# Products with the tokens on the output's partitions: 512 columns at a time from chunks of half the rows

## The chip, the cores and the metric

The kernel runs on one core of a Trainium2 chip. The metric is the device time of one execution in microseconds (us). TensorE (PE) multiplies, VectorE (DVE) and ScalarE (ACT) evaluate and convert, GpSimd (POOL) does some element-wise work, SyncE (SP) issues most of the DMAs.

## The reference, cut to what matters

Two layers of a hybrid network run over 256 tokens (`x`) and 256 context tokens (`ctx`); layer 0 updates both, layer 1 only the first. All products are 1024 wide on the reduced side (`D_MODEL = 1024`).

```python
mod = silu(c) @ ada_w[i] + ada_b[i]            # 6 * 1024 columns
h   = modulate(rmsnorm(x, norm1_g), sh1, sc1)
p   = h @ w_in                                 # 7168 columns:
# u, v of the gating (512 + 512), q, k, v of attention (3 * 512),
# three parts of the long convolution (3 * 512), three gates (3 * 1024)
a    = u * (w_s @ rmsnorm(v) + b_s)            # gating over tokens
attn = softmax(q k^T + bias) v                 # 8 heads of 64
hy   = two long convolutions, by Fourier transforms
m    = g_a * (a @ wb0) + g_b * (attn @ wb1) + g_c * (hy @ wb2)
x    = x + g1 * (m @ w_out)
x    = x + g2 * (gelu(conv(h2 @ up_a)) * (h2 @ up_b)) @ down
```

## The kernel before

Nearly every product is done with the features on the output's partitions: a piece of the weight, 128 x 128, is the stationary operand, and all tokens (512 in layer 0, 256 in layer 1) stream past it. To keep fp32 accuracy each operand is split in a high and a low part (ACT casts the high part, L251, DVE subtracts, L258), and three matmuls are made for each piece: low times high, high times high, high times low (L311 to L313). Tiles of the split weights are called `wp`, those of the activations `hh` and `hl`, the accumulators `mm`.

Two products are made the other way round, with the tokens on the partitions: `v` of the gating (4 tiles of 128 tokens in layer 0, 2 in layer 1) and `v` of attention (`va`, 4 tiles in both). There the activations are stationary and the weights stream (`tm_use`, L940 to L957, accumulators `mt`, L951 to L953). A load brings 1024 rows by 256 columns of the weight, so a tile takes 24 matmuls of 256 columns, and ACT writes each half of 256 columns out (L954).

The order of the work is written out by hand. `items` is a list of weight chunks (`dense`), of the chunks of the modulation's weights (`native`, function `ada`, L373: one chunk is 128 rows by 2048 columns, used as it is, and makes four matmuls of 512 columns) and of calls. `run_items` (L222) walks through it, loads three chunks ahead, and splits the weights `AHEAD` = 4 (layer 0) or 6 parts ahead. A chunk is cut into parts by `cuts` (L209).

Beside this list run the side works: gating (`sgu`), the filters, the convolution (`hyena`), attention. Each is a generator whose steps are pieces of work. They wait in the queue `side`, and `pump` (L155) makes one step of the first of them. In layer 0 a step is made after every accumulated tile of 512 tokens: 24 matmuls for a gate or a q, k tile, 12 for a tile of a branch product (L329: `ctl["pace"]`), after two tiles of `tm_use`, and after every `ada`. So it is the list that spaces the steps of the side works. The attention's loop (L848) makes one of six kinds of step in turn: in steps 0, 1, 3 and 5 of six it makes `scores` (matmuls `S`, then on DVE a bias, the maximum `mx`, on ACT the exponential, on DVE the division, giving two tiles `P_`); in steps 2 and 4 `stack` prepares the next heads' `K_` and `Q_` by turns on ACT and DVE; one step after its scores, `P_` is transposed by TensorE (`PT`); later `values` multiplies (`pv`). I count these steps from 0 in layer 0.

The chunk of `ada` with ch = 1 takes 8 of these units and the one with ch = 2 another 8, all in layer 0. Before the change they stand behind the six chunks of the convolution's parts, behind the four chunks of q and k, behind the two of `va`, and behind the first four gates. An `ada` chunk holds one of the four accumulator buffers (pool `psm`) from its first unit to its eighth. The gates and the branch products alternate (`LEAD` = 2 gates ahead).

Of the kernel before, what the change touches and what calls it, by code (L numbers as in the profile page):

```python
# [11 lines left out]
F32 = mybir.dt.float32  # L12
F32R = mybir.dt.float32r
AF = mybir.ActivationFunctionType
# [5 lines left out]
KD = 8  # L20
# [73 lines left out]
def trunk_kernel(ctx: ExitStack, tc: tile.TileContext, A: dict, out: bass.AP):  # L94
    nc = tc.nc
    mm, act, vec, pool = nc.tensor.matmul, nc.scalar.activation, nc.vector, nc.gpsimd
# [5 lines left out]
    psm = ctx.enter_context(tc.tile_pool(name="psm", bufs=4, space=PSUM))  # L102
# [3 lines left out]
    def U(name, dt=F32):  # L106
        return unit.tile([128, 512], dt, tag="u", name=name)

    def fm(name, n, T, dt=F32):

        if T == 512:
            return [U(name, dt) for _ in range(n)]
        r = []
        for _ in range((n + 1) // 2):
            u = U(name, dt)
            r += [u[:, 0:256], u[:, 256:512]]
        return r[:n]
# [37 lines left out]
    def pump(n=1):  # L155
        for _ in range(n):
            if not side:
                return
            try:
                next(side[0])  # L160
            except StopIteration:
                side.popleft()
# [8 lines left out]
    def start(g):  # L171
        side.append(g)
        return g
# [32 lines left out]
    def dense(src, kt, ncols, use, kind="m"):  # L206
        items.append((kind, src, kt, ncols, use))

    def cuts(kind, kt, ncols):  # L209


        if kind == "m":
            return [[(k, min(k + 4, kt), c, c + 128) for k in range(0, kt, 4)] for c in range(0, ncols, 128)]
        return [[(k, k + 2, 0, ncols) for k in range(0, kt, 2)]]

    def native(src, use):
        items.append(("n", src, 0, 0, use))

    def call(f, wait=True):
        items.append(("c", None, wait, 0, f))  # L220

    def run_items():  # L222
# [4 lines left out]
        for n, i in enumerate(loads):  # L227
            for j, ps in enumerate(cuts(*items[i][0:1], *items[i][2:4])):
                parts += [(n, i, q) for q in ps]
                last[i, j] = len(parts)  # L230
# [44 lines left out]
        for i, it in enumerate(items):  # L275
            if it[0] == "c":
                if it[2]:
                    flush()
                it[4]()
                continue  # L280
            if it[0] == "n":
                if i not in raw:
                    load_native()
                it[4](raw.pop(i))
                load_native()
                continue
            load_to(pos + RAWB + (not nats))
            qs = cuts(it[0], it[2], it[3])

            def piece(j, more=True, i=i, qs=qs):  # L290

                n = last[i, j]
                ahead = ctl["ahead"] if more else 0
                hi_to(n + ahead + (2 if more else 0))
                advance()
                lo_to(n + ahead)
                ctl["at"] = n
                W = []
                for m, (k0, k1, c0, c1) in enumerate(qs[j]):
                    h, l_ = spl.pop(n - len(qs[j]) + m)  # L300
                    W += [(h[:, k], l_[:, k]) for k in range(k1 - k0)]
                return W
            it[4](piece)
            pos += 1
# [30 lines left out]
    def fm_chunk(R, segs, evac, nm=2):  # L335

        def use(piece):
            for m in range(nm):
                W = piece(m)
                for (s0, s1) in segs:  # L340
                    fm_run([(W, evac, m)], R, s0, s1)
        return use
# [30 lines left out]
    def ada(l, ch, k):  # L373
        src = A["ada_w"][l, k * 128:(k + 1) * 128, ch * 2048:(ch + 1) * 2048]

        def use(w):
            if k == 0:
                ada.ps = psm.tile([128, 512], F32, tag="m", name="ada")
            ps = ada.ps
            v = w.rearrange("p (t j i) -> p j t i", j=4, i=32)  # L380
            for j in range(4):
                mm(ps[32 * j:32 * j + 32, :], lhsT=scc[:, k, :], rhs=v[:, j], start=(k == 0), stop=(k == KD - 1),  # L382
                   tile_position=(0, 32 * j))
            if k == KD - 1:
                ada_evac(l, ch, ps)
            pump()
        native(src, use)
# [33 lines left out]
    def ada_evac(l, ch, ps):  # L421

        tr = U("adat")
        vec.transpose(out=tr, in_=ps)
        t0 = ch * 16
        b = prm[:, P_AB + 48 * l + t0:P_AB + 48 * l + t0 + 16].unsqueeze(2).to_broadcast([128, 16, 2])
        vec.tensor_tensor(out=mod[l][:, t0:t0 + 16, :], in0=tr.rearrange("p (t i) -> p t i", i=32)[:, :, 0:2], in1=b,
                          op=ALU.add)
        if ch != 1:
            w_, g_ = (0, P_N1) if ch == 0 else (1, P_N2)  # L430
            sc = mod[l][:, 8 + 24 * w_:16 + 24 * w_, :]
            g = prm[:, g_ + 8 * l:g_ + 8 * l + 8].unsqueeze(2).to_broadcast([128, KD, 2])
            vec.scalar_tensor_tensor(out=gs[l][:, w_], in0=sc, scalar=1.0, in1=g, op0=ALU.add, op1=ALU.mult)
# [442 lines left out]
    def layer(l):  # L876
        nseg = 2 if l < DEPTH - 1 else 1
        T = 256 * nseg
        full = [(0, T)]
        S = {}  # L880
        w_in = A["w_in"][l].rearrange("(k p) n -> p k n", p=128)

        def col(c0, n=256):
            return w_in[:, :, c0:c0 + n]
# [35 lines left out]
        def late(f):  # L920

            def use(piece):
                f()(piece)
            return use
# [12 lines left out]
            else:  # L937
                dense(col(c * 256), KD, 256, late(lambda c=c: fm_edge(S["H"], halves, u_evac(c), 2, st1, 4, NH1[1])))

        def tm_use(c, ntt, dst, func):  # L940

            def use(piece):
                W = piece(0)
                rh, rl = S["H"]
                for t in range(ntt):
                    ps = psm.tile([128, 512], F32, tag="m", name="mt")
                    o = ps[:, 0:256]
                    for k in range(KD):
                        wh, wl = W[k]
                        x, y = rh[k][:, t * 128:(t + 1) * 128], rl[k][:, t * 128:(t + 1) * 128]  # L950
                        mm(o, lhsT=x, rhs=wl, start=(k == 0), stop=False)  # L951
                        mm(o, lhsT=x, rhs=wh, start=False, stop=False)  # L952
                        mm(o, lhsT=y, rhs=wh, start=False, stop=(k == KD - 1))  # L953
                    act(out=S[dst][t][:, c * 256:(c + 1) * 256], in_=o, func=func)  # L954
                    if t % ctl["pace"][2] == ctl["pace"][2] - 1:
                        pump()
            return use  # L957

        for c in range(2):
            dense(col(512 + c * 256), KD, 256, tm_use(c, 2 * nseg, "v", AF.Gelu), "t")  # L960

        def go_sgu():
            S["sgu"] = start(sgu(l, nseg, S["u"], S["v"]))
# [29 lines left out]
        ada_todo = [(l, ch, k) for ch in (1, 2) for k in range(KD)] if l == 0 else []  # L993
# [11 lines left out]
        def qk_evac(i, c):  # L1005
            def ev(m, ps, s0, s1):
                for s in range(s1 // 256):
                    act(out=S["qk"][s, c * 2 + m][:, i * 256:(i + 1) * 256], in_=ps[:, s * 256:(s + 1) * 256], func=AF.Copy,
                        scale=1.0 if i else HD ** -0.5)
            return ev  # L1010

        def qkv_chunks():
            def alloc():
                S["qk"] = {(s, m): U("qk") for s in range(2) for m in range(4)}
                S["va"] = [U("va") for _ in range(4)]
            call(alloc, False)
            for i, c0, segs in ((0, 1024, full), (1, 1536, [(0, 512)])):
                for c in range(2):
                    dense(col(c0 + c * 256), KD, 256,
                          late(lambda c=c, i=i, sg=segs: fm_chunk(S["H"], sg, qk_evac(i, c))))  # L1020
                    if ada_todo:
                        ada(*ada_todo.pop(0))

            def go():
                S["o"] = fm("o", 4, T)
                S["at"] = start(attention(l, S["qk"], S["va"], S["o"], nseg))
                next(S["at"])
            call(go)
            for c in range(2):
                dense(col(2048 + c * 256), KD, 256, tm_use(c, 4, "va", AF.Copy), "t")  # L1030
                if ada_todo:
                    ada(*ada_todo.pop(0))

        hy_chunks()
        qkv_chunks()


# [327 lines left out]
    for l in range(DEPTH):  # L1365
        layer(l)
# [94 lines left out]
```

## Time and profile before

| | |
|---|---|
| time, median of 3 runs | 1459.46 us (1457.94 to 1460.45) |
| the profiled execution | 1458.98 us |
| its span | 1457.1 us |
| PE busy | 1414.2 us (97%) |
| DVE busy | 1012.2 us (69%) |
| ACT busy | 660.7 us (45%) |
| mean granted clock of TensorE | 0.993 |

A matmul's listed duration overlaps with that of the next one; what it takes from TensorE is the distance between the starts of two matmuls in an unbroken stream. Idle time of PE is what the others cost.

### The profile page before, as it was taken

The page shows a single profiled execution, that of the slowest core. Times are in us where ns is not written, and L with a number is a line of the kernel's source. Part 1 is how long each engine was busy: PE and PEld are TensorE (multiplying, and loading weights), DVE is VectorE, ACT ScalarE, POOL GpSimd, SP SyncE. Part 2 cuts the span into 40 slices and gives each one's busy share as a digit, 9 for nine tenths or more (in the row PEclk, how much of TensorE's full clock was granted, in tenths as well). Part 3 has the DMA queues.
Part 4 walks back from the last instruction along what each step waited for, and adds up shares of the span by engine and source line. Part 5 has one row for each costly group of instructions (what it writes and reads, how often), then busy time and mean ns, then how long its engine had stood idle before and what let it go on. Part 6 is the DMA issues. An engine that isn't in the chain of part 4 may idle for free.

```text
span 1457.1 us, 22092 instructions
## 1 busy us (share of the span) xinstructions
PE 1414.2 (97%) x8742; PEld 1216.3 (83%) x8742; DVE 1012.2 (69%) x1872; ACT 660.7 (45%) x1362; POOL 92.4 (6%) x96
## 2 busy tenths in 40 slices
PE   4999999999999999999999999999999999999997
PEld 2887777767787889988878787899789899899997
DVE  6736744676775567667978898577767787776574
ACT  4442332434664335433313433465336755665352
POOL 1010201010000000000011120000110000000000
PEclk9999999999999999999999999999999999999998
DMA  9934435233222432334578535545233445556642
GB/s 317 301 131 162 130 131 177 101 114 125 80 87 89 157 105 98 116 116 144 165 242 260 185 122 176 164 141 164 87 116 117 148 157 195 166 175 173 200 142 66
DMA packets 194531, 220.17 MB, mean 151 GB/s; under 512 B 5531, under 2 KB 182716, under 8 KB 189308
## 3 DMA queue, kind: packets, MB, share of 16 engines
q1 hardware_dynamic: 189420, 206.97, 44.0%
q0 software_dynamic: 2896, 9.18, 2.0%
q10 hardware_dynamic: 2112, 2.62, 0.7%
q8 instruction: 68, 1.11, 0.3%
q14 instruction: 35, 0.29, 0.1%
HBM read 215.61 MB, written 1.05 MB: 149 GB/s over the span
## 4 chain that ended last, share of the span: by engine, by line
PE 85%; DVE 7%; ACT 3%; issue 1%; ACTq 0%; POOL 0%; DMA 0%; DVEq 0%; POOLq 0%
PE mm L311 23%; PE mm L313 23%; PE mm L312 23%; PE mt L951 1%; PE mt L953 1%; PE mt L952 1%; DVE wp L258 1%; PE PT L807 1%; PE pv L820 1%; PE S L783 1%; PE ada L382 1%; PE Ze L643 1%; PE Zo L644 1%; PE mm L316 1%; PE mm L317 1%
## 5 line engine op out<-in xcount | busy, mean ns | idle before, releaser
L311 PE MATMUL mm<-hl,wp 128*128 128x256 f32 (+1 forms) x1476 | 500.2, 339 | 0.8 <-DVE hl L485 0.7
L313 PE MATMUL mm<-hh,wp 128*128 128x256 f32 (+1 forms) x1476 | 491.6, 333 | 0.5 <-DVE wp L258 0.5
L312 PE MATMUL mm<-hh,wp 128*128 128x256 f32 (+1 forms) x1476 | 491.2, 333 | 0.0
L258 DVE TENSOR_TENSOR wp<-w,wp 128x512 fp32r<-128x512 f32 (+1 forms) x576 | 374.9, 694 | 27.4 <-ACT wp L251 25.0
L251 ACT CAST wp<-w 128x512 fp32r<-128x512 f32 (+1 forms) x576 | 321.3, 610 | 83.4 <-DMA w<-ffn_w_down 34.5
L311 PEld LDWEIGHTS mm<-hl,wp 128*128 128x128 f32 x1476 | 280.3, 190 | 37.9 <-issue 7.0
L312 PEld LDWEIGHTS mm<-hh,wp 128*128 128x128 f32 x1476 | 280.4, 190 | 29.1 <-issue 2.9
L313 PEld LDWEIGHTS mm<-hh,wp 128*128 128x128 f32 x1476 | 280.2, 190 | 28.8 <-DVE wp L258 1.2
L311 PE MATMUL mm<-ml,wp 128*128 128x256 f32 (+1 forms) x392 | 126.1, 322 | 0.0
L313 PE MATMUL mm<-mh,wp 128*128 128x256 f32 (+1 forms) x392 | 125.4, 320 | 0.0
L312 PE MATMUL mm<-mh,wp 128*128 128x256 f32 (+1 forms) x392 | 125.4, 320 | 0.0
L311 PEld LDWEIGHTS mm<-ml,wp 128*128 128x128 f32 x392 | 74.7, 190 | 7.7 <-issue 2.4
L313 PEld LDWEIGHTS mm<-mh,wp 128*128 128x128 f32 x392 | 74.7, 190 | 5.4
L312 PEld LDWEIGHTS mm<-mh,wp 128*128 128x128 f32 x392 | 74.7, 191 | 5.3
L405 DVE SCALAR_TENSOR_TENSOR acc<-wn,scc,acc 128x512 f32<-128x512 f32 x112 | 78.4, 766 | 0.0
L1110 DVE SCALAR_TENSOR_TENSOR xT<-mm,mod,xT 128x256 f32<-128x256 f32 x72 | 33.7, 481 | 63.0 <-PE mm L313 61.5
L1144 ACT ACTIVATE a<-mm,prm 128x256 f32<-128x256 f32 (+1 forms) x48 | 30.8, 643 | 89.5 <-PE mm L313 88.3
L988 DVE SCALAR_TENSOR_TENSOR a<-mm,prm,a 128x255 f32<-128x255 f32 (+1 forms) x48 | 27.9, 582 | 56.4 <-ACT a L1144 56.4
L311 PE MATMUL mm<-bl,wp 128*128 128x512 f32 (+1 forms) x192 | 65.4, 341 | 0.0
L312 PE MATMUL mm<-bh,wp 128*128 128x512 f32 (+1 forms) x192 | 64.6, 336 | 0.0
L313 PE MATMUL mm<-bh,wp 128*128 128x512 f32 (+1 forms) x192 | 64.6, 336 | 0.0
L951 PE MATMUL mt<-wp,hh 128*128 128x256 f32 x224 | 64.2, 286 | 0.1
(620 smaller groups left out, 2043.9 us busy)
## 6 DMA issues: line engine op xcount, KB each, us to landing
w<-w_in SPq DMA_DIRECT2D x56, 1024.0 KB, 5.2
w<-ffn_w_up SPq DMA_DIRECT2D x44, 1024.0 KB, 5.2
wn<-ada_w SPq DMA_DIRECT2D x40, 1024.0 KB, 4.9
w<-w_branch SPq DMA_DIRECT2D x24, 512.0 KB, 3.4
w<-ffn_w_down SPq DMA_DIRECT2D x16, 768.0 KB, 5.1
w<-ffn_w_down SPq DMA_DIRECT2D x16, 640.0 KB, 4.4
aw<-ada_w SPq DMA_DIRECT2D x32, 256.0 KB, 6.0
w<-w_out SPq DMA_DIRECT2D x8, 1024.0 KB, 5.3
```

What stands on the lines that cost most here:

```text
L251: nc.scalar.copy(h, src)
L258: vec.tensor_tensor(out=l_, in0=src, in1=spl[st["lo"]][0], op=ALU.subtract)
L311: mm(o, lhsT=wh, rhs=rl, start=(k == 0), stop=False)
L312: mm(o, lhsT=wh, rhs=rh, start=False, stop=False)
L313: mm(o, lhsT=wl, rhs=rh, start=False, stop=(k == n - 1))
L316: mm(o, lhsT=w[k][0], rhs=rh, start=(k == 0), stop=False)
L317: mm(o, lhsT=w[k][1], rhs=rh, start=False, stop=False)
L405: vec.scalar_tensor_tensor(out=o, in0=v[:, j], scalar=scc[:, k, m:m + 1], in1=o, op0=ALU.mult, op1=ALU.add)
L951: mm(o, lhsT=x, rhs=wl, start=(k == 0), stop=False)
L988: vec.scalar_tensor_tensor(out=yv[:, :, 1:256], in0=pv[:, :, 0:255], scalar=w[:, 0:1], in1=yv[:, :, 1:256], op0=ALU.mult, op1=ALU.add)
L1110: vec.scalar_tensor_tensor(out=xs, in0=ps[:, s * 256 - s0:(s + 1) * 256 - s0], scalar=mod[l][:, gate_t + t, s:s + 1], in1=xs, op0=ALU.mult ...
L1144: act(out=y, in_=ps[:, 0:s1 - s0], func=AF.Identity, scale=w[:, 1:2], bias=b)
```

## The change

`tm_use` now takes chunks of 512 columns by 512 rows (half of the reduced side) instead of 256 columns by 1024 rows. The first chunk opens one accumulator of 512 columns for each tile of tokens and leaves it open; the second adds the other half of the rows and then writes the tile out, 512 columns at once. `cuts` makes parts of one row block by 512 columns. A tile thus takes 12 matmuls of 512 columns in each of the two chunks. All four accumulator buffers are open in `va`, so no `ada` may be open there: the second group of `ada` (ch = 2) begins in the gates, one behind each of gates 0 to 7, and none stands behind the k chunks and the `va` chunks any more.

```diff
-        return [[(k, k + 2, 0, ncols) for k in range(0, kt, 2)]]
+        n = 512 // ncols
+        return [[(k, k + n, 0, ncols) for k in range(0, kt, n)]]
...
-        def tm_use(c, ntt, dst, func):
+        def tm_use(h, ntt, dst, func, tiles):
...
                 for t in range(ntt):
-                    ps = psm.tile([128, 512], F32, tag="m", name="mt")
-                    o = ps[:, 0:256]
-                    for k in range(KD):
-                        wh, wl = W[k]
+                    if h == 0:
+                        tiles.append(psm.tile([128, 512], F32, tag="m", name="mt"))
+                    for i, (wh, wl) in enumerate(W):
+                        k = 4 * h + i
                         x, y = rh[k][:, t * 128:(t + 1) * 128], rl[k][:, t * 128:(t + 1) * 128]
-                        mm(o, lhsT=x, rhs=wl, start=(k == 0), stop=False)
-                        mm(o, lhsT=x, rhs=wh, start=False, stop=False)
-                        mm(o, lhsT=y, rhs=wh, start=False, stop=(k == KD - 1))
-                    act(out=S[dst][t][:, c * 256:(c + 1) * 256], in_=o, func=func)
+                        mm(tiles[t], lhsT=x, rhs=wl, start=(k == 0), stop=False)
+                        mm(tiles[t], lhsT=x, rhs=wh, start=False, stop=False)
+                        mm(tiles[t], lhsT=y, rhs=wh, start=False, stop=(k == KD - 1))
+                    if h:
+                        act(out=S[dst][t], in_=tiles[t], func=func)
...
-        for c in range(2):
-            dense(col(512 + c * 256), KD, 256, tm_use(c, 2 * nseg, "v", AF.Gelu), "t")
+        def tm_chunks(c0, ntt, dst, func):
+            tiles = []
+            for h in range(2):
+                dense(w_in[:, 4 * h:4 * h + 4, c0:c0 + 512], 4, 512, tm_use(h, ntt, dst, func, tiles), "t")
+
+        tm_chunks(512, 2 * nseg, "v", AF.Gelu)
...
-                    if ada_todo:
+                    if ada_todo and i == 0:
                         ada(*ada_todo.pop(0))
...
-            for c in range(2):
-                dense(col(2048 + c * 256), KD, 256, tm_use(c, 4, "va", AF.Copy), "t")
-                if ada_todo:
-                    ada(*ada_todo.pop(0))
+            tm_chunks(2048, 4, "va", AF.Copy)
```

How it moves the order on TensorE, in layer 0's attention, steps 9 and 10. The score matmuls `S` of step 9 give the two tiles `P_` that the transposes `PT` of step 10 read. Before, the 24 matmuls of a gate's tile stand between them:

```order
L820 MATMUL pv<-PTs,va 64x256 x8
L783 MATMUL S<-K__3101,Q__3210 128x256 x4
L311 MATMUL mm<-hl,wp 128x512
L312 MATMUL mm<-hh,wp 128x512
...
L313 MATMUL mm<-hh,wp 128x512
L807 MATMUL PT<-ident,P__3499 128x128
L807 MATMUL PT<-ident,P__3507 128x128
```

In the changed kernel, where the lines of these functions are one and of `tm_use` one to three numbers higher, the same two steps are:

```order
L821 MATMUL pv<-PTs,va 64x256 x8
L784 MATMUL S<-K__2943,Q__3070 128x256 x4
L383 MATMUL ada<-wn,scc 32x512 x4
L808 MATMUL PT<-ident,P__3363 128x128
L808 MATMUL PT<-ident,P__3371 128x128
```

One unit of `ada` stands where the gate's tile stood, since its step follows the gate's second tile.

On DVE, steps 10 and 11 of the same loop: `stack` (K_, Q_), then the maxima `mx` of step 11. Before, two splits `wp` stand between them:

```order
L762 TENSOR_TENSOR K__3449<-qk,K__3449 64x256
L767 TENSOR_TENSOR Q__3576<-qk,Q__3576 64x256
L762 TENSOR_TENSOR K__3457<-qk,K__3457 64x256
L767 TENSOR_TENSOR Q__3583<-qk,Q__3583 64x256
L258 TENSOR_TENSOR wp<-w,wp 128x512 x2
L790 TENSOR_REDUCE mx<-S 128x1 x2
```

In the changed kernel the tile between these steps is one of a branch product, with its split and its two-part evaluation (`gt`, `m`):

```order
L763 TENSOR_TENSOR K__3297<-qk,K__3297 64x256
L768 TENSOR_TENSOR Q__3390<-qk,Q__3390 64x256
L763 TENSOR_TENSOR K__3305<-qk,K__3305 64x256
L768 TENSOR_TENSOR Q__3397<-qk,Q__3397 64x256
L259 TENSOR_TENSOR wp<-w,wp 128x512
L1069 SCALAR_TENSOR_TENSOR gt<-gt,mm 128x512
L1070 TENSOR_TENSOR m<-m,gt 128x512
L791 TENSOR_REDUCE mx<-S 128x1 x2
```

The steps of attention are the same in both; what lies between them, on TensorE and on DVE, is not.

## Rows read from the trace of the kernel before

**Rows 1.** The page: busy time by engine (share of the span) and count.
```profile
PE 1414.2 (97%) x8742; PEld 1216.3 (83%) x8742; DVE 1012.2 (69%) x1872; ACT 660.7 (45%) x1362; POOL 92.4 (6%) x96
```

**Rows 2.** Groups by line and form: count, busy us, mean ns.
```profile
L951 PE MATMUL mt<-wp,hh 128*128 128x256 f32 x224 | 64.2, 286 | 0.1
```

**Rows 3.** Timeline of PE (start, us, line), 256 columns, first and last of 95.
```profile
236.87 0.28 PE L952 MATMUL mt<-wp,hh 128*128 128x256 f32 x1
...
248.14 0.28 PE L953 MATMUL mt<-wp,hl 128*128 128x256 f32 x1
```

**Rows 4.** Timeline of PE, 512 columns, first and last of 17.
```profile
228.27 0.39 PE L312 MATMUL mm<-hh,wp 128*128 128x512 f32 x1
...
231.90 0.39 PE L313 MATMUL mm<-hh,wp 128*128 128x512 f32 x1
```

**Rows 5.** Timeline of PE, layer 0: a gate's tile, one `ada`, the next tile.
```profile
293.22 0.39 PE L313 MATMUL mm<-hh,wp 128*128 128x512 f32 x1
293.54 1.07 PE L382 MATMUL ada<-wn,scc 128*32 128x512 f32 x8
...
294.88 0.39 PE L312 MATMUL mm<-hh,wp 128*128 128x512 f32 x1
```

**Rows 6.** Timeline of PE and DVE, attention step 1.
```profile
347.00 0.39 PE L311 MATMUL mm<-hl,wp 128*128 128x512 f32 x1
...
350.97 0.49 DVE L796 TENSOR_SCALAR P__3038<-P__3038,sm 128x512 f32<-128x512 f32 x1
```

**Rows 7.** Timeline, end of attention step 2 to step 4.
```profile
358.86 1.95 PE L820 MATMUL pv<-PTs,va 128*64 128x256 f32 x16
...
361.31 0.40 PE L311 MATMUL mm<-bl,wp 128*128 128x512 f32 x1
...
363.00 0.35 DVE L796 TENSOR_SCALAR P__3175<-P__3175,sm 128x256 f32<-128x256 f32 x1
```

**Rows 8.** Timeline, steps 16 to 18: transposes, `stack`, the next probabilities.
```profile
431.77 0.27 PE L807 MATMUL PT<-ident,P__3886 128*128 128x128 f32 x1
...
435.30 0.42 DVE L767 TENSOR_TENSOR Q__3929<-qk,Q__3929 64x256 fp32r<-64x256 f32 x1
...
439.40 0.35 DVE L796 TENSOR_SCALAR P__3967<-P__3967,sm 128x256 f32<-128x256 f32 x1
```

**Rows 9.** Timeline, step 14: last transpose, last piece of `stack`.
```profile
420.60 0.27 PE L807 MATMUL PT<-ident,P__3754 128*128 128x128 f32 x1
...
424.14 0.42 DVE L767 TENSOR_TENSOR Q__3823<-qk,Q__3823 64x256 fp32r<-64x256 f32 x1
```

**Rows 10.** Timeline, steps 7 to 9: PE's wait, ACT's issue of DMAs, `bh`.
```profile
386.57 0.33 PE L807 MATMUL PT<-ident,P__3404 128*128 128x128 f32 x1 [0.57 <-DVE P__3404 L796]
...
387.54 0.62 ACT L251 CAST wp<-w 128x512 fp32r<-128x512 f32 x1 [1.75 <-issue]
...
395.57 2.18 ACT L177 CAST bh<-pc 128x512 fp32r<-128x512 f32 x4
```

**Rows 11.** Timeline of DVE, the evaluation of one finished `ada` chunk.
```profile
337.83 0.72 DVE L424 STREAM_TRANSPOSE adat<-ada 128x512 f32<-128x512 f32 x1 [0.27 <-PE ada L382]
...
338.80 0.18 DVE L433 SCALAR_TENSOR_TENSOR gs<-mod,prm 128x16 f32<-128x16 f32 x1
```

**Rows 12.** Timeline of DVE, the convolution between its transforms.
```profile
282.80 0.69 DVE L647 TENSOR_TENSOR T<-te,Zo 128x512 f32<-128x512 f32 x1 [0.43 <-PE Zo L644]
...
294.62 0.69 DVE L666 TENSOR_TENSOR P<-yr 128x512 f32<-128x512 f32 x1
```

**Rows 13.** Timeline of PE, both layers: the waits before the inverse transforms.
```profile
326.40 0.46 PE L690 MATMUL yT<-kst,P 128*128 128x128 f32 x2 [1.67 <-DVE P L666]
...
1065.56 0.46 PE L690 MATMUL yT<-kst,P 128*128 128x128 f32 x2 [1.71 <-ACT wp L251]
```

**Rows 14.** Windows round these waits: busy by engine, then PEclk, DMA share, GB/s.
```profile
320.00:340.00 20.00, 18.05 (x95) 14.00 (x94) 13.62 (x25) 3.54 (x7) 1.28 (x3) 1.00 0.36 119
1060.00:1080.00 20.00, 18.01 (x116) 16.46 (x116) 11.73 (x20) 4.25 (x11) 2.91 (x3) 0.91 0.38 112
```

## The prediction

> **What bounds the kernel now.** I read the page first: TensorE is busy for 97% of the span, far more than any other engine [rows 1]. So the end is set by the stream of matmuls, and a change pays in two coins only: what the stream itself takes, and the waits that interrupt it. Next I read the groups by line and form for the products that change: the line L951 occurs 224 times with 256 columns [rows 2], and its two sister lines as often, 672 matmuls in all. Their listed 286 ns are no cost, since they overlap; the timeline gives the cost as the distance of the starts. Then I listed the places where TensorE waits, in the timeline from 230 to 480 us and again in layer 1, because the change moves four units of `ada`, and every unit makes a step of the side works.
>
> **The stream.** In 256 columns, 94 distances take 248.14 - 236.87 = 11.27 us, 119.9 ns each [rows 3]; in 512 columns, 16 distances take 231.90 - 228.27 = 3.63 us, 226.9 ns each [rows 4]. Both are of unbroken stretches at the full clock. One matmul of 512 replaces two of 256: 239.8 - 226.9 = 12.9 ns gained, 336 times: 4.3 us. The same operands are stationary and moving as before, in the same pattern (each stationary piece is loaded anew for every matmul in both), so I take the rate of rows 4 as it is. The bounds are 0 (two halves cost one whole) and 4.3.
>
> The Trainium skill (TensorE: Matmul & The Clock Gate, section on the back-to-back issue gap) gives N/2.4 + 2.5 ns for the distance of isolated matmuls at full clock: 109.2 and 215.8 ns, so 2.5 ns a pair and an estimated 0.8 us instead of 4.3. Rows 3 and 4 show some 11 ns more per matmul at both widths, so here the rule understates what a halved count saves.
>
> **What costs nothing.** Loads, splits and their sizes stay (1 MB a chunk, four parts of 128 x 512); a split waits for no more data than before. Writing out 512 columns at once is one ACT instruction for two, on an engine that is busy for 45% [rows 1]. The four open accumulators: the first tile of the next product needs the buffer of tile 0, which is written out three tiles, 36 matmuls or 8.2 us, earlier. If ACT were late by more than that, the excess would be the price; I take 0. The loads of `ada` come one per gate and branch, each issued by SP when the unit before it has been used, some 18 us ahead; DMA was busy for about a third of such stretches [rows 14]. On POOL nothing is added.
>
> **The moved units.** Four units leave the q/k/va stretch for gates 4 to 7, which lie in layer 0's attention. One occupies TensorE from a tile's last matmul at 293.22 to the second of the next at 294.88, less two distances of 0.227: 1.2 us [rows 5]. TensorE pays that in either place. What is new is the step behind each: the attention's steps used to be 12 or 24 matmuls apart (2.7 or 5.45 us), now three of them are 1.2 us apart, and the whole pattern of 12s and 24s is shifted against the steps. I went through steps 0 to 16, with the order of the changed kernel for what is queued and rows of before for how long it takes. Four chains are needed.
>
> - Scores after another score step: the matmul behind `S` starts at 347.00, the second `P_` is ready at 350.97 + 0.49 = 351.46: 4.46 us [rows 6].
> - Scores of step 3, with DVE free: 361.31 to 363.35, 2.04 us [rows 7]. There `pv` and `S` together take TensorE 361.31 - 358.86 = 2.45 us, of it 1.95 `pv` and 0.5 `S`.
> - `stack` after the transposes: 431.77 to 435.72, 3.95 us, and until the next `P_` are ready with a branch tile's work in between, 439.75 - 431.77 = 7.98 us [rows 8]; after a full transposition 420.60 to 424.56, 3.96 us [rows 9].
> - DVE's evaluation of a finished `ada`, 337.83 to 338.98: 1.15 us [rows 11].
>
> Now the new waits of TensorE, need less cover:
>
> - Steps 1 to 2: 4.46 against 12 matmuls, 2.72 (before: 24): 1.7 us.
> - Steps 4 to 6: `stack` 3.95 and a free chain 2.04 make 6.0; cover 1.2 + 0.5 + 2.72 = 4.4: 1.6 us.
> - Steps 8 to 10: in front of `stack` ACT has the issue of four DMAs (1.75) and the four casts `bh` (2.18) [rows 10], some 3 us net of its head start; then 3.96, two splits 1.2, the chain 2.04: 10.2. Cover: 24 matmuls 5.45, `pv` and `S` 2.45, one `ada` 1.2, 9.1: 1.1 us from the transposes' end, and up to 3.6 without the head start. I take 2.1.
> - Steps 10 to 12: 7.98 against 2.72 + 0.5 + 2.72 = 5.9: 2.0 us.
> - Steps 14 to 16: 3.96 + 1.15 + 2.04 = 7.2 against 1.2 + 2.45 + 2.72 = 6.4: 0.8 us.
> - Steps 7 to 8 get 24 matmuls in place of 12: the wait of 0.57 [rows 10] goes.
>
> That is +7.6 us. From step 16 on the order is that of before. If DVE and ACT work ahead where I queue them, only the first of these is sure (1.7), less 0.6; if nothing overlaps, it is 10.
>
> **The convolution.** Its chain on DVE takes 282.80 to 295.31, 12.5 us [rows 12]. One more of its four passages gets 24 + `ada` + 24 matmuls of cover, 12.1 us, where it had 24 more: +0.4. The last passage has that cover in both, and waits 1.67 us in the trace [rows 13]; that stays. Bounds: 0 and 1.7.
>
> **The sum.** -4.3 + 7.6 + 0.4 = +3.7, so 1458.98 + 3.7 = 1462.7 us. The profiled execution is 0.5 us under the median of the three runs; I forecast 1463.0. In layer 1 no step moves; its third of the streaming gain is in the 4.3.
>
> **Rivals.**
>
> 1. *Attention's chains hide* (DVE and ACT, at 69 and 45%, keep up). For it: DVE idles a third of the span. Against it: the chains are latencies in a fixed order, and even now TensorE waits at 12 matmuls [rows 10]. Then -4.3 + 1.1 + 0.4 = -2.8 at the least hidden, -4.3 fully: 1455 to 1456.5.
> 2. *The clock falls in the new waits.* In layer 1 the wait of 1.71 us is followed by a stretch at a granted 0.91, that is part of it at the lower level, 1.2 GHz; the wait of 1.67 in layer 0 stayed at 1.00 [rows 13, 14]. 0.09 of 20 us is 1.8 us a time. One or two such falls in the five new waits: +5.5 to +7.3, 1464.5 to 1466.5. The fall in layer 1 may as well vanish, since the starts move; that is 1.8 the other way, for any case.
> 3. *The stream gains only the page's 0.8*: everything else as forecast, +7.2, 1466. The rows speak against it.
> 4. *The open accumulators block.* `ada` holds one buffer during gates 4 to 7, leaving three for gates and branches; a branch tile that DVE evaluates late by more than two tiles (5.4 us) would stop TensorE. From then on each such tile costs the excess, perhaps 1 us: 1464 to 1467. In the trace the same three buffers served the first gates without such a wait.
>
> **Chances.** The forecast (waits of 5 to 10 us) 0.50, of it 0.33 slower by over 0.2% (2.9 us, about what a measurement of this kernel tells from no change) and 0.17 within; rival 1 0.28 (0.19 faster, 0.09 within); rival 2 0.14 (slower but for 0.01); rivals 3 and 4 0.08 (0.06 slower, 0.01 within, 0.01 faster). Faster 0.20, same 0.28, slower 0.52. The range from 1455.5 (rival 1 in the main) to 1468 (the upper bound of the waits, or the forecast with two falls) leaves about 0.1 on each side. The forecast's own range is 1460 to 1467.
>
> **What would show it.** Right: `mt` matmuls of 512 columns 227 ns apart in 336 instances; in layer 0's attention TensorE waits for DVE at the transposes of steps 2, 6, 10 and 12, 7 us more than before in all; none at step 8. Wrong: those transposes start without idle time (rival 1, time under 1457), a granted clock under 1.00 between 340 and 440 us (rival 2), matmuls of the products over 235 ns apart (rival 3), or matmuls `mm` that wait for DVE's L1069 or ACT's L1059 (rival 4).

## The result, and the profile after

The changed kernel takes 1474.3 us (median of four runs, 1472.8 to 1475.4), the kernel before 1458.7 beside it: 1.0103 times the time, 95% interval 1.0091 to 1.0115. That is 15.6 us slower, where the sum gave 3.7 (1463.0 us), and above the range that was given. The direction was right; one term of the sum was far off, and without what it left out the direction would not have come out (below).

TensorE's own work is as long as before [rows 1], in a longer span (1471.0 for 1457.1 us); what is new is nearly all idle time. The page of the changed kernel, busy time by engine:

```profile
PE 1413.2 (96%) x8406; PEld 1199.5 (82%) x8406; DVE 1012.9 (69%) x1872; ACT 659.8 (45%) x1348; POOL 92.2 (6%) x96
```

The stream does what was forecast [rows 2 to 4]. The groups of the changed kernel hold the products of 512 columns, 112 times a line, 336 in all:

```profile
L952 PE MATMUL mt<-wp,hh 128*128 128x512 f32 x112 | 44.7, 399 | 0.0
```

The median distance of their starts is 227 ns in each of the four products, where it was 120 ns for 256 columns; the 96 of the gating's `v` in layer 0 take 21.76 us (first start to last, and one distance for the last), the 192 of before 23.03. That is 13 ns for each matmul of 512 columns; 336 x 13 ns, 4.4 us, are gained.

The loss lies between two matmuls that both kernels have, the first `nsum` after 150 us and one where the feed-forward part begins. Timeline of PE in the changed kernel (start, us, line, operation, idle before and what ended it):

```profile
159.06 0.38 PE L582 MATMUL nsum<-ones,tot 128*128 128x2 f32 x2 [0.73 <-POOL tot L569]
...
310.42 2.05 PE L677 MATMUL y<-P,kst 128*128 128x512 f32 x2 [8.46 <-DVE P L667]
...
339.81 0.46 PE L691 MATMUL yT<-kst,P 128*128 128x128 f32 x2 [2.92 <-DVE P L667]
...
368.01 0.30 PE L808 MATMUL PT<-ident,P__2891 128*128 128x128 f32 x1 [0.77 <-DVE P__2891 L797]
...
368.86 0.33 PE L808 MATMUL PT<-ident,P__2900 128*128 128x128 f32 x1 [0.55 <-DVE P__2900 L797]
...
389.18 0.30 PE L808 MATMUL PT<-ident,P__3092 128*128 128x128 f32 x1 [1.00 <-DVE sm L796]
...
413.44 0.30 PE L808 MATMUL PT<-ident,P__3363 128*128 128x128 f32 x1 [1.34 <-DVE sm L796]
...
421.70 0.30 PE L808 MATMUL PT<-ident,P__3431 128*128 128x128 f32 x1 [1.39 <-DVE sm L796]
...
444.86 0.30 PE L808 MATMUL PT<-ident,P__3668 128*128 128x128 f32 x1 [0.24 <-DVE sm L796]
...
585.81 0.38 PE L312 MATMUL mm<-hl,wp 128*128 128x256 f32 x1 [0.56 <-DVE hl L486]
```

The stretch takes 585.81 - 159.06 = 426.75 us. In the kernel before, the same two stand at 162.19 and 572.05: 409.86. The six waits at `PT` are those forecast for the attention, 5.3 us, and the wait of 0.57 [rows 10] is gone. The wait of 8.46 us at `y` (third of the four convolution passages, the first of segment 1) was in no term of the sum; that at `yT` of the fourth passage grew from 1.67 [rows 13] to 2.92.

The windows of the changed kernel show what follows the two (busy by engine, then PEclk, DMA share, GB/s):

```profile
306.00:312.00 6.00, 1.58 (x2) 0.84 (x3) 5.96 (x11) 1.69 (x3) 0.00 (x0) 0.59 0.00 0
312.00:318.00 6.00, 6.00 (x18) 3.33 (x17) 3.86 (x7) 0.78 (x2) 0.00 (x0) 0.84 0.53 178
...
336.00:342.00 6.00, 2.85 (x12) 1.76 (x12) 5.96 (x11) 1.76 (x3) 0.00 (x0) 0.94 0.00 0
342.00:348.00 6.00, 6.00 (x27) 5.23 (x27) 2.63 (x6) 0.00 (x0) 0.00 (x0) 0.78 0.64 215
```

After each wait some 3 us of matmuls run at the lower level, 1.2 GHz: the first `y` take 2.05 us for two. Estimated from what the four windows lack of the full clock, counted only where TensorE is at work (about 0.8, 1.0, 0.3 and 1.3 us), that costs 3.4 us. The rows bear it out: the same eight matmuls `y`, and the first sixteen of `yT` with three products behind them, take 3.2 us less in experiment 4, where the clock stays at 1.00. In the same places the kernel before has 1.00 throughout.

Sum for the stretch: waits of the convolution 8.46 + 2.92 - 1.67 = 9.7; attention 5.3 - 0.6 = 4.7; clock 3.4; stream of `va` (96 x 13 ns) -1.2: 16.6 of the 16.9 us. Outside the stretch the other 240 matmuls of 512 columns gain 3.1 us, and 16.9 - 3.1 = 13.8 is what the profiled execution (1472.81 us, the fastest of the four) takes more than that of before; between the medians it is 15.6.

Why does `P` come late? DVE, ACT and POOL before the wait at `y`, changed kernel:

```profile
289.91 0.69 DVE L648 TENSOR_TENSOR T<-te,Zo 128x512 f32<-128x512 f32 x1 [0.42 <-PE Zo L645]
...
292.61 0.69 DVE L259 TENSOR_TENSOR wp<-w,wp 128x512 fp32r<-128x512 f32 x1 [1.41 <-PE mm L314]
...
295.10 0.69 DVE L259 TENSOR_TENSOR wp<-w,wp 128x512 fp32r<-128x512 f32 x1 [1.80 <-PE mm L313]
...
299.10 1.29 POOL L657 TENSOR_TENSOR m<-T,K 128x512 f32<-128x512 f32 x1 [33.53 <-PE mm L313]
299.28 1.66 DVE L658 TENSOR_TENSOR yr<-P,K 128x512 f32<-128x512 f32 x1 [3.48 <-PE mm L314]
...
301.77 0.69 DVE L659 TENSOR_TENSOR yi<-P,K 128x512 f32<-128x512 f32 x1 [0.84 <-PE mm L313]
...
305.26 0.68 DVE L658 TENSOR_TENSOR yr<-Pp,K 128x512 f32<-128x512 f32 x1
...
306.62 0.62 ACT L252 CAST wp<-w 128x512 fp32r<-128x512 f32 x1 [10.69 <-DVE yi L659]
...
309.58 0.69 DVE L667 TENSOR_TENSOR P<-yr 128x512 f32<-128x512 f32 x1
```

From the start of `T` to the start of `P` it is 309.58 - 289.91 = 19.7 us, against 11.8 before [rows 12]; to the end of `P`, as the prediction counted, 20.4 against 12.5. The products `m`, `yr`, `yi` read nothing that TensorE's `mm` makes: `P`, `T` and `K` are there since 291 us. They wait for a *place*. `mm` at L313 and L314 reads weight parts `wp`; `yr` takes the buffer of one. Following the buffers through the two programs gives, for the two halves of the third passage, how many of the 77 shared buffers hold something when `yr` is written (`yr` among them), which tile had its buffer, and how many matmuls the program has between that tile's last read and the new writer:

```
kernel     half  held  buffer's last tile   matmuls since its last read
before     1     72    tm (read by PE)      25
before     2     73    m2 (read by DVE)     16
changed    1     77    wp (read by PE)       1
changed    2     75    K  (read by DVE)      0
```

In the changed kernel, the third passage's products come behind `br_split` of the first branch, which has taken eight buffers for `bh` and `bl` (the high and low parts of the branch's input); six hold `gt` by then, eight weight parts. For the first half nothing is free but what TensorE has just read, so DVE goes at TensorE's pace, and TensorE then waits for DVE.

Theory A: four lost steps of the side works move the third passage behind `br_split`, where the shared buffers are all held. Rival B: the passage has less cover, whatever the buffers. Rival C: the wide chunks, or the accumulator that `ada` holds in gates 4 to 7, cause the waits.

### The profile page after: what moved, and what is told of

Same layout as the page of the kernel before. It is cut to its first block, busy times and chain, and to the rows that moved or that the text cites. A ratio compares the mean times of both kernels' runs of the same rounds, so it can differ in the third digit from the quotient of the medians.

```text
span 1471.0 us, 21413 instructions
## 1 busy us (share of the span) xinstructions
PE 1413.2 (96%) x8406; PEld 1199.5 (82%) x8406; DVE 1012.9 (69%) x1872; ACT 659.8 (45%) x1348; POOL 92.2 (6%) x96
## 4 chain that ended last, share of the span: by engine, by line
PE 82%; DVE 10%; ACT 3%; issue 2%; ACTq 0%; POOL 0%; DVEq 0%; POOLq 0%
PE mm L312 22%; PE mm L314 22%; PE mm L313 22%; DVE wp L259 2%; PE mt L953 2%; PE mt L952 2%; PE mt L954 2%; DVE mx L791 1%; PE PT L808 1%; PE ada L383 1%; PE pv L821 1%; PE Zo L645 1%; PE Ze L644 1%; PE mm L317 1%; PE mm L318 1%
## 5 line engine op out<-in xcount | busy, mean ns | idle before, releaser
L314 PE MATMUL mm<-hh,wp 128*128 128x256 f32 (+1 forms) x1476 | 491.7, 333 | 1.2 <-DVE wp L259 1.2
L313 PE MATMUL mm<-hh,wp 128*128 128x256 f32 (+1 forms) x1476 | 491.5, 333 | 0.0
L252 ACT CAST wp<-w 128x512 fp32r<-128x512 f32 (+1 forms) x576 | 321.6, 610 | 102.5 <-DMA w<-ffn_w_down 35.3
L313 PEld LDWEIGHTS mm<-hh,wp 128*128 128x128 f32 x1476 | 280.5, 190 | 29.6 <-issue 3.1
L314 PEld LDWEIGHTS mm<-hh,wp 128*128 128x128 f32 x1476 | 280.3, 190 | 29.7 <-DVE wp L259 2.3
L314 PE MATMUL mm<-mh,wp 128*128 128x256 f32 (+1 forms) x392 | 125.4, 320 | 0.0
L313 PE MATMUL mm<-mh,wp 128*128 128x256 f32 (+1 forms) x392 | 125.4, 320 | 0.0
L314 PEld LDWEIGHTS mm<-mh,wp 128*128 128x128 f32 x392 | 74.7, 190 | 5.4
L313 PEld LDWEIGHTS mm<-mh,wp 128*128 128x128 f32 x392 | 74.7, 190 | 5.3
L313 PE MATMUL mm<-bh,wp 128*128 128x512 f32 (+1 forms) x192 | 64.6, 336 | 0.0
L314 PE MATMUL mm<-bh,wp 128*128 128x512 f32 (+1 forms) x192 | 64.6, 336 | 0.0
L1059 ACT ACTIVATE gt<-mm 128x512 f32<-128x512 f32 (+1 forms) x48 | 23.5, 490 | 78.1 <-PE mm L314 78.0
```

The costliest lines, as they stand in the source:

```text
L252: nc.scalar.copy(h, src)
L313: mm(o, lhsT=wh, rhs=rh, start=False, stop=False)
L314: mm(o, lhsT=wl, rhs=rh, start=False, stop=(k == n - 1))
```

## Experiments

Intervals are 95%, ratios to the kernel before; "stretch" is the distance of the two matmuls above. The expectations count a wait from the last matmul's start plus 0.23 us, so that they have 8.6 and 3.1 us for the 8.46 and 2.92 of the rows; their 6.3 us for the attention include two waits of some 0.5 us that the kernel before has as well.

**1. All four steps back.** `ada` gets an argument that leaves its step out; the places in the q/k/va stretch issue a step alone.

```diff
-                    if ada_todo and i == 0:
-                        ada(*ada_todo.pop(0))
+                    if ada_todo and i == 0:
+                        ada(*ada_todo.pop(0))
+                    elif ada_todo:
+                        call(pump, False)
...
                 dense(w_in[:, 4 * h:4 * h + 4, c0:c0 + 512], 4, 512, tm_use(h, ntt, dst, func, tiles), "t")
+                if dst == "va" and ada_todo:
+                    call(pump, False)
...
-                    ada(*ada_todo.pop(0))
+                    ada(*ada_todo.pop(0), i < 4)
```

> The changed kernel, in which each of the four places between the q/k/va chunks that lost their ada unit issues one step of the side works all the same, and the four units in gates 4 to 7 issue none. So every step stands where it stood before the change, while the units themselves and the 512-column products stay as changed. Theory A (steps that come late put the third convolution passage behind the branch's input split, where all 77 shared buffers are taken): the waits of 8.6 and 3.1 us at y and yT and those of the attention go, only the stream's gain of 4.3 us is left: 1454 to 1455 us. Theory B (the convolution has too little cover beside the moved units' matmuls, whatever the buffers): the same. Theory C (the wide chunks, or the accumulator that ada holds in gates 4 to 7, cause the waits): 1470 to 1475, with the wait at y still there.

1456.2 us, ratio 0.9977 (0.9967 to 0.9986): 3.4 us under the kernel before. The wait at `y` is gone, the attention's new ones are gone, and C with them. That 1454 to 1455 was missed has a place: behind `yT`, where TensorE waits as long as in the kernel before, the clock now falls (0.78 of 318 to 324 us, 0.94 of the next 6, some 1.7 us). Timeline of PE, then the windows:

```profile
293.46 1.02 PE L678 MATMUL y<-P,kst 128*128 128x512 f32 x2
...
319.75 0.46 PE L692 MATMUL yT<-kst,P 128*128 128x128 f32 x2 [1.68 <-DVE P L668]
```

```profile
318.00:324.00 6.00, 4.04 (x18) 3.43 (x18) 4.62 (x8) 1.62 (x3) 0.00 (x0) 0.78 0.53 177
324.00:330.00 6.00, 6.00 (x27) 4.92 (x27) 1.96 (x4) 0.10 (x1) 0.64 (x2) 0.94 0.41 129
```

**2. and 3. Either half of it.** Experiment 2 has only the last hunk (no steps with the units in gates 4 to 7), experiment 3 only the others (steps in q/k/va, and those in the gates too).

> The changed kernel, in which the four moved ada units issue no step in gates 4 to 7; the steps in the q/k/va stretch stay lost. Theories A and B: the convolution keeps its waits (about 11.7 us and the lower clock behind them), the attention's steps stand 12 or 24 matmuls apart again, so that most of its 6.3 us of waits go: 1467 to 1470 us. If the two sets of waits are not separate, it stays at 1474.

> The changed kernel with one step in each of the four places of the q/k/va stretch that lost their ada unit; the units in gates 4 to 7 keep their steps too, so there are four steps more than before. Theories A and B: the convolution's waits are gone (some 12 us and the lower clock behind them, 2 to 3), the attention still gets steps one unit (1.2 us) apart and keeps waits of 4 to 8 us: 1458 to 1462 us. Theory C: 1470 to 1475.

Experiment 2: 1473.9 us, 1.0098 (1.0076 to 1.0120), outside its expectation, and at the 1474 that was named for the case that the two sets of waits hang together. The trace gives another reason. The waits at `y` and `yT` are as in the changed kernel, to the hundredth; the attention's new ones are gone from their places, but its steps are now too few, and the rest is run without cover ahead of the last branch, with two new waits and a clock of 0.91 from 480 to 500 us:

```profile
314.75 2.05 PE L678 MATMUL y<-P,kst 128*128 128x512 f32 x2 [8.46 <-DVE P L668]
...
489.10 0.30 PE L809 MATMUL PT<-ident,P__4090 128*128 128x128 f32 x1 [1.56 <-DVE sm L797]
...
492.05 0.30 PE L809 MATMUL PT<-ident,P__4117 128*128 128x128 f32 x1 [1.56 <-DVE sm L797]
```

Experiment 3: 1460.9 us, 1.0010 (1.0000 to 1.0021), as expected. No wait at `y`; the stretch is 414.8 us against 408.3 in experiment 1, so steps one `ada` apart cost the attention about 6.6 us here, 1.7 of it a clock of 0.83 from 405 to 415 us (both kernels have the fall behind `yT`). Between experiment 3 and the changed kernel lie 426.8 - 414.8 = 12 us, near the 13.1 that the convolution's waits and clock add up to; it is no exact share, since the attention's waits differ as well.

**4. More shared buffers.**

```diff
-NU = 77
-RAWB = 3
+NU = 81
+RAWB = 2
```

> The changed kernel with 81 shared buffers in place of 77; the room comes from the raw weights, of which 3 chunks instead of 4 are held. No step moves. Theory A: where the third passage of the convolution took the buffer of a weight part that TensorE had still to read, it now takes one read 13 matmuls earlier; the wait of 8.6 us at y shrinks to under 2 and the lower clock behind it goes: 1461 to 1466 us. Theory B: the chain is as long as before, the wait stays, 1473 to 1475. If the raw weights come late with 3 held, SP's queue shows it as waits of the splits spread over the whole run, and the time rises everywhere.

The whole run is slower, 1488.4 us (1.0202, 1.0183 to 1.0221), outside the range for A; that late raw weights would slow the whole run had been named. The place in dispute answers the question. The first half's `yr` now takes a buffer that was read 13 matmuls before. Timeline of PE, and DVE between:

```profile
291.66 0.69 DVE L648 TENSOR_TENSOR T<-te,Zo 128x512 f32<-128x512 f32 x1 [0.42 <-ACT te L647]
...
304.70 0.68 DVE L667 TENSOR_TENSOR P<-yr 128x512 f32<-128x512 f32 x1
...
305.53 1.10 PE L677 MATMUL y<-P,kst 128*128 128x512 f32 x2 [1.82 <-DVE P L667]
...
331.82 0.46 PE L691 MATMUL yT<-kst,P 128*128 128x128 f32 x2 [1.58 <-DVE P L667]
```

13.0 us from `T` to `P`, 1.82 us of wait, and the clock stays at 1.00 through 296 to 350 us. Two of DVE's products are as slow there as in the changed kernel (1.66 us, beside POOL's), so POOL isn't what made the chain long. The stretch falls from 426.8 to 415.7 us. The total is lost from 570 us on, with three chunks of raw weights: ACT waits for DMAs before its casts of weight parts. Groups of the changed kernel, then of this one:

```profile
L252 ACT CAST wp<-w 128x512 fp32r<-128x512 f32 x560 | 316.6, 616 | 102.5 <-DMA w<-ffn_w_down 35.3 <-DMA w<-ffn_w_up 25.9 <-DVE yi L659 10.7
```

```profile
L252 ACT CAST wp<-w 128x512 fp32r<-128x512 f32 x560 | 316.8, 617 | 267.8 <-DMA w<-ffn_w_up 110.4 <-DMA w<-ffn_w_down 90.1 <-DMA w<-w_in 43.8
```

**6. Fewer weight parts held**, the same question with the raw weights left alone.

```diff
-AHEAD = (4, 6)
+AHEAD = (2, 6)
```

> The changed kernel with layer 0's weights split 2 parts ahead instead of 4, so that about four fewer of the 77 shared buffers are held by weight parts; raw weights and steps as in the changed kernel. In the third convolution passage the products then take buffers last read 13 to 16 matmuls earlier instead of 1. Theory A: the wait at y falls from 8.6 us to 1.5 to 2.5, that at yT from 3.1 to about 1.8, the half clock behind them goes; 10 to 11 us less, 1462 to 1466 us, unless splits come late elsewhere in layer 0. Theory B: the chain is as long as before and the waits stay, 1473 to 1476.

At `y` and `yT` the same waits as in experiment 4; the clock stays at 1.00 behind `y` and falls behind `yT` (0.72 of 336 to 342 us):

```profile
308.45 1.10 PE L677 MATMUL y<-P,kst 128*128 128x512 f32 x2 [1.82 <-DVE P L667]
...
334.73 0.46 PE L691 MATMUL yT<-kst,P 128*128 128x128 f32 x2 [1.57 <-DVE P L667]
...
830.56 0.79 PE L314 MATMUL mm<-mh,wp 128*128 128x512 f32 x1 [6.15 <-DVE wp L259]
...
928.00 0.80 PE L314 MATMUL mm<-hh,wp 128*128 128x512 f32 x1 [6.33 <-DVE wp L259]
```

The total is the worst of all, 1522.0 us (1.0435, 1.0405 to 1.0465): the last two rows are of many in layer 0's later parts, where splits now come late, as the expectation had allowed for. Two different ways of freeing buffers, neither of which moves a step, take the same 6.6 us out of the wait at `y`; A holds, and B is left with at most the 1.82 us that remain.

**5. The kernel before with four steps lost, and nothing else.**

```diff
-                    if ada_todo:
-                        ada(*ada_todo.pop(0))
+                    if ada_todo:
+                        ada(*ada_todo.pop(0), i == 0)
...
                 if ada_todo:
-                    ada(*ada_todo.pop(0))
+                    ada(*ada_todo.pop(0), False)
```

> The kernel before with one thing changed: the four ada units between the k and va chunks issue no step of the side works. The units stay where they are, the products stay at 256 columns. Theories A and B: this alone brings the waits at y (8 to 9 us) and yT (about 3) and the half clock behind them, and the run is that of the changed kernel without the stream's gain: 1475 to 1479 us. Theory C (wide chunks, or ada's accumulator held in gates 4 to 7): 1458 to 1461.

1477.2 us (1.0121, 1.0102 to 1.0140), with the very wait:

```profile
319.50 2.05 PE L677 MATMUL y<-P,kst 128*128 128x512 f32 x2 [8.46 <-DVE P L667]
```

**8. The units moved, products at 256 columns.** The kernel before, with `if ada_todo and i == 0` in the q/k chunks and no `ada` behind the va chunks.

> The kernel before (products at 256 columns) with the ada units moved as in the change. Theories A and B: all of the loss and nothing of the stream's gain: 1477 to 1480 us. Theory C, that the wide chunks have part in the waits: 1460 to 1470. The difference to the changed kernel is what the 512-column stream gains: 4.3 us by the distances of the matmuls, 0.8 by the rule of rival 3.

1480.0 us (1.0136, 1.0116 to 1.0156), with 8.46 us at `y` again. The 512-column stream thus makes the changed kernel 0.0033 x 1459 = 4.8 us faster than this (some 3.4 us either way, by the two intervals), and, between experiments 5 and 2, 3.4 us (some 4.2 either way). Both stand near the 4.3 by the distances, but the second alone doesn't exclude 0.8.

**7. The kernel before with 74 buffers.**

```diff
-NU = 77
+NU = 74
```

> The kernel before with 74 shared buffers instead of 77; nothing else. Theory A from the other side: the fourth convolution passage then takes a buffer that TensorE read 2 matmuls earlier (13 before), and weight parts get theirs later, so the wait at yT of 1.8 us grows to 2.5 to 6 us: 1460 to 1466 us. Theory B: nothing moves, 1458 to 1460.

1463.4 us (1.0023, 1.0013 to 1.0033), inside the range, but not by the mechanism that was written. (The reuse named there is in the third passage, and it brought no wait at `y`.) The wait at the fourth passage's `yT` shrank to 1.22; new is one of 1.12 at the second passage's `yT` (271.25 us) and one of 1.40 in the feed-forward part. Fewer buffers cost time, but this run doesn't show the wait in dispute: a buffer read two matmuls before does not make it alone. In this kernel the third passage still has 24 matmuls more of cover than in the changed one.

**9. and 10. Three, and two, of the four steps kept** in the q/k/va stretch; the steps left out come in gate 4 (and 5), so that the attention still gets all its steps. The edit of experiment 1, for three steps with `c < 3`, `2 + h < 3` and `i < 5` in its conditions, for two with `c < 2`, `2 + h < 2` and `i < 6`.

> As the kernel with all four steps back, but only the first three of the four places in the q/k/va stretch issue a step; the one left out comes in gate 4 instead, so that the number of steps is the same. Theory A: all products of the third convolution passage still come ahead of the branch's input split and take buffers read 13 matmuls or more earlier; no wait at y, 1455 to 1459 us. If the loss grows with every lost step (cover alone), a quarter of it: 1459 to 1462.

> Two of the four places in the q/k/va stretch issue a step, the other two steps come in gates 4 and 5. Theory A: the second half of the third passage's products now comes behind the branch's input split, with 77 buffers taken, and takes one that TensorE reads 1 matmul earlier; the first half does not. A wait of 2 to 5 us at y (against 8.6 with both halves behind), 1459 to 1466 us. Cover alone: half of the loss, spread over the passages, without a wait of more than 2 us at y.

Two kept: 1459.3 us (1.0004, 0.9994 to 1.0013). The second half of the third passage lies behind `br_split`, and the wait is there, a quarter of the size:

```profile
301.92 1.10 PE L678 MATMUL y<-P,kst 128*128 128x512 f32 x2 [2.14 <-DVE P L668]
...
353.37 0.30 PE L809 MATMUL PT<-ident,P__2865 128*128 128x128 f32 x1 [1.55 <-DVE P__2865 L798]
```

Three kept: 1449.7 us, ratio 0.9937 (0.9921 to 0.9954), 9.2 us faster than the kernel before by the ratio, and the fastest kernel of all. It beats its expectation by 5 us. The whole third passage is still ahead of `br_split`, and the fourth, one step later than in experiment 1, has one tile more of cover, so that its wait at `yT` is gone as well:

```profile
295.64 1.02 PE L678 MATMUL y<-P,kst 128*128 128x512 f32 x2
...
320.06 0.38 PE L692 MATMUL yT<-kst,P 128*128 128x128 f32 x2
```

Its windows hold a clock of 1.00 from 300 to 480 us, and its stretch is 402.6 us, against 408.3 with four steps kept and 409.9 in the kernel before. So the loss doesn't grow with each lost step: one lost gains 5.7 us, two lose 4.1 (to experiment 1), four that come nowhere else lose 17.3 (experiment 2).

**11. Four steps kept, 78 buffers** (`NU = 78`).

> The kernel with all four steps back and 78 shared buffers instead of 77, which fit without giving up anything. Theory A: with the steps in their old places the buffers are not what TensorE waits for, so one more changes nothing by itself: 1454 to 1457 us, within 2 us of the same with 77.

1455.8 us (0.9974, 0.9964 to 0.9983), that is the time of experiment 1.

## Why the prediction was wrong

- **The stream, -4.3**: right. 227 ns as in the rows taken for it. The rule of rival 3 gave 0.8; the distances speak against it, and so does experiment 1, where all steps are back and 3.4 us (2.0 to 4.8) are gained in spite of a fall of the clock. Experiments 8 and 5 (4.8 and 3.4 us) agree with 4.3, with wider intervals.
- **The attention, +7.6**: right in its mechanism and its places, somewhat too large. Steps 1 to 2 measured 1.32 for 1.7, 4 to 6 1.00 for 1.6, 8 to 10 1.34 for 2.1, 10 to 12 1.39 for 2.0, 14 to 16 0.24 for 0.8; the wait before step 8 went as said. That makes 4.7 us for 7.6; DVE works ahead a little more than was allowed for. The upper 3.6 given for steps 8 to 10 doesn't follow from its rows: issue and casts in full (1.75 + 2.18) make the chain 11.1 us, 2.0 over the cover.
- **The convolution, +0.4 with bounds 0 and 1.7**: the step that failed. The cover was right: from 289.26 to the wait TensorE has 12.5 us of work, where 12.1 were forecast. The chain was not. It was taken as 12.5 us wherever it stands [rows 12], but moved behind `br_split` it took 20.4, since its products found no free buffer. Measured 9.7 us in waits and 3.4 in clock. Of the waits, experiments 4 and 6 give 8.0 to the buffers (6.6 at `y`, 1.3 at `yT`) and leave 1.7, the upper bound that had been given for the smaller cover; not all of that is cover, since the chain is still 13.7 us in experiment 4. "The last passage has that cover in both" failed for the same reason.
- **What costs nothing**: this list asked of TensorE's accumulators whether there were enough of them (there were; rival 4 didn't come), and not of the 77 shared buffers in SBUF, which the same moved steps load differently. The Trainium skill (Perfetto Trace Analysis, Optimization Strategy) says that the same gap, repeated on the engine that should be full, can mean that SBUF or PSUM has no room for the next tile. The trace agrees in the cause, though here it is one gap of 8.46 us and a smaller one, 2.92, a passage later.
- **The direction** was right by luck. The stream and the attention as measured add up to -4.4 + 4.7 = +0.3 us, no change that a run could tell; what made the kernel slower is the term that stood at +0.4.
- **Rival 2**, the clock falling in new waits, came true as a part: twice, behind the convolution's waits, 3.4 us in sum. It hangs on the failed step, not on the attention, where it had been put.

What stays open: what of the wait at `y` each of the early stalls on DVE carries (the two `wp` at 292.61 and 295.10, the `yr` at 299.28), and why the clock falls behind some of the shorter waits and not behind others (below).

## What to carry to other kernels

Where work is moved in a program that hands out buffers from one pool, a chain's duration doesn't move with it: at the new place, count what is held, and look who read the buffer that the moved instruction will be given. A wait of DVE for TensorE at an instruction that reads nothing of TensorE's is the sign in a trace. And a step that is lost with the unit that carried it is an edit of its own: here the lost and moved steps made the loss, while the rest of the change was worth 3.4 us, and 9.2 with one of the four steps put later.

## What the hardware showed beside

- The lower clock doesn't follow from a wait's length alone. TensorE waited 1.67 us at the fourth passage's `yT` in the kernel before and the clock stayed at 1.00; 1.68 us at the same matmul in experiment 1 was followed by a window of 0.78. At that matmul 1.58 us in experiment 4 was followed by no fall, 1.57 us in experiment 6 by a window of 0.72.
- The same product on DVE, 128 x 512, takes 0.68 us by itself (`yr` at 305.26) and 1.66 (`yr` at 299.28) where POOL's product runs beside it (`m` at 299.10). The Trainium skill (Advanced Engine Details and Errata, GPSIMD Details) says that POOL and DVE share an SBUF interface, with conflicts for DVE instructions that have two SBUF inputs; these rows agree.
- Holding three chunks of raw weights in place of four (experiment 4) raises ACT's idle time before its weight casts from 102.5 to 267.8 us.
